# Expert weights in a fixed ring of eight buffers, context weights through GpSimd's queue, expert outputs combined by pairs

## The chip, the cores and the metric

The kernel runs on one core of a Trainium2 chip, in fp32. The metric is the device time of one execution in microseconds (us), as the median of several runs. TensorE (PE) has two clock levels, 1.2 and 2.4 GHz; the profile gives the granted clock of a stretch as a share of the upper one. PE's weight loads have an engine name of their own (PEld). DVE is VectorE, ACT is ScalarE, POOL is GpSimd, and SP is SyncE, which here only issues DMAs.

## What is computed

Two model blocks run one after the other on a latent sequence `x` and a context sequence `ctx_2` of 256 tokens each. The first block ends with a mixture of 32 experts, the second begins with a mixer that needs the projections of its own context. Cut to what matters here:

```python
def hier_moe(h, wg, bg, we, be, w_gate, w_up, w_down):     # 4 groups x 8 experts, top 2 of one group
    ...
    for gi in range(N_GROUPS):
        hid = (jax.nn.silu(jnp.einsum('td,edf->tef', t, w_gate[gi]))
               * jnp.einsum('td,edf->tef', t, w_up[gi])
               * combine[:, gi, :, None].astype(t.dtype))
        out = out + jnp.einsum('tef,efd->td', hid, w_down[gi])
    return out.reshape(B, L, D).astype(h.dtype)
...
# block 2, layer 0: the context's part does not depend on block 1
hc = modulate_2(rmsnorm(ctx, norm1_g[layer]), csh1, csc1)
cx = project_in(hc, w_in)
...
c_f, s_f = chunked_gated_linear_attention(cq, ck, cv, ca_f, zero, False)
```

The width is 1024, an expert's hidden width 512, and the 32 experts have 192 MB of fp32 weights, all of which are read.

## The kernel before

**The expert stage.** The function `moe` takes the 32 experts in 16 pairs `q`. The tokens of two pairs (a quad, `qd`) are gathered at once (`dispatch`). For a pair, `gate_up(q)` multiplies eight 1 MB chunks of gate and up weights, and `down(q - 1)` four chunks of the pair before; the two experts of a pair stand on the two halves of PE's columns, so their matmuls come in twos. Between its parts the code calls `step()`, which runs one piece of the list `todo` (gathering the next quad, adding up a finished one), and, for q > 0, `next(ctx, None)`.

**The context in between.** `ctx` is the generator `context()`: the context's part of block 2, layer 0. Each `yield` ends a piece, and one piece is run after each of the four sub-steps of a `gate_up`. It loads `ctx_2`, normalises and transposes it, and then multiplies it by nine blocks of `w_in_2` (1 MB where they have 256 columns, 512 KB where 128, 128 KB where 32). `weights_c` splits a block into a high and a low part, `whi` by a cast on ACT and `wlo` by a subtraction on DVE (`s.split`), and asks for the next one (`s.raw`). Then come four gated heads; each begins with a matmul `tr<-dTc,upst`, a chain of DVE and ACT operations that ends in `de`, one `yield`, and the transposes of `de`.

**Buffers and queues.** All 192 expert chunks are loaded by `chunk(i)` on SP's queue in a fixed order. A chunk goes to one of six buffers: three of the rotating pool buffers `raw`, another `raw` in `moe`'s own pool, and the two halves `rawh` of `h0`. The context's blocks are loaded by SP too, into the same three rotating `raw` buffers. SP works in order: a load whose buffer is not yet free holds up all that stand behind it.

**Adding up.** `down` leaves the outputs of two pairs in `yh` and `yl` (high and low part); `combine(qd)` multiplies them by the selection matrix in four parts of eight matmuls each and adds the result to `xT`, once for every two pairs. The parts stand at the end of `todo`.

Of the kernel before, what the change touches and what calls it, by code (L numbers as in the profile page):

```python
# [17 lines left out]
P = 128  # L18
D = 1024
# [999 lines left out]
def moe(s):  # L1019
    nc, tc, I = s.nc, s.tc, s.I  # L1020
    mt = nc.tensor.matmul
    CAP = s.cap
    with tc.tile_pool(name="pm", bufs=1) as pool_:
        pool = Pool(pool_, {"xg": 2, "raw": 1, "t1": 4, "kq": 4, "sel": 2, "selT": 3, "hT": 2, "ws": 4, "glo": 2, "sq": 2},
                    {"nt": "sq", "adarow2": "glo"})
# [109 lines left out]
        for _ in range(2):  # L1135
# [10 lines left out]
                 [(q - 1, u, j) for u in (4, 5) for j in range(2) if q > 0]]  # L1146
        first = [(s.wp, "raw")] * 3 + [(pool, "raw")] + [(s.wp, "whi"), (s.wp, "wlo")] * 2
        big = []

        def chunk(i):  # L1150

            if i >= 8:
                n = 4 + (i - 8) % 2 if i < 10 else (i - 10) % 6 if i < 184 else (i - 184) % 4
            if i < 8 or n < 4:
                p_, tag = first[i if i < 8 else n]
                t = p_.tile([P, 2048], F32, tag=tag, name="raw")
            else:

                if not big:
                    big.append(s.xp.tile([P, 2, 2048], F32, tag="h0", name="rawh"))  # L1160
                t = big[0][:, n - 4]
# [6 lines left out]
        pre = s.pre + [chunk(i) for i in range(3, 8)]  # L1168
        made = 8

# [49 lines left out]
        nc.vector.tensor_tensor(wsq[:, :, 1], s.fng, s.fng, op=OP.mult)  # L1220
        yh = pool.tile([P, 2, D], F32R, name="yh")
        yl = pool.tile([P, 2, D], F32R, tag="yl", name="yl")
        quads = {}
# [85 lines left out]
        def down(q, hT, then):  # L1309
            i = q % 2  # L1310
# [12 lines left out]
            for c in range(2):  # L1323
                sl = slice(512 * c, 512 * c + 512)
                nc.scalar.copy(yh[:, i, sl], pd[c])
                nc.vector.tensor_tensor(yl[:, i, sl], pd[c], yh[:, i, sl], op=OP.subtract)

        def combine(qd):
            _, selT, _ = quads.pop(qd)

            def part(c):
                po = s.at((P, 2, T))
                for j in range(2):
                    sl = slice((c + j) * P, (c + j + 1) * P)
                    for y in (yh, yl):
                        for i in range(2):
                            mt(po[:, j], y[:, i, sl], selT[:, i], start=y is yh and i == 0, stop=y is yl and i == 1)
                for j in range(2):
                    s.hold = nc.vector.scalar_tensor_tensor(s.xT[:, c + j], po[:, j], s.gt2[:, c + j:c + j + 1],
                                                            s.xT[:, c + j], op0=OP.mult, op1=OP.add).ins  # L1340
                if qd == 7:

# [15 lines left out]

            return [lambda c=c: (last if qd == 7 else part)(c) for c in range(0, 8, 2)]

# [5 lines left out]
        def load_context():  # L1366
            s.ctx2 = s.raw(I["ctx_2"][0].rearrange("(a p) d -> p a d", p=P))
# [4 lines left out]
        def context():  # L1372


            load_context()
            kb = pool.tile([P, 512], F32, name="kbc")
# [36 lines left out]
            cols += [(3072, 256), (3328, 256)]  # L1413
            raws = [s.raw(w2[:, :, c:c + n]) for c, n in cols[:1]]

            def weights_c():

                w = s.split(None, raws.pop(0))
                cols.pop(0)
                if cols:  # L1420
                    raws.append(s.raw(w2[:, :, cols[0][0]:cols[0][0] + cols[0][1]]))
                return w

# [24 lines left out]
            for hp in range(2):  # L1448
# [12 lines left out]
                for j in range(2):  # L1461
# [30 lines left out]
                    nc.vector.tensor_tensor(cu, cu, kst, op=OP.mult)  # L1492
                    yield
                    pt = s.tr((P, 4, P))
# [21 lines left out]
                    for i in range(4):  # L1516
                        for d in range(2):
# [41 lines left out]
        for q in range(17):  # L1559
# [11 lines left out]
            if q == 16:  # L1571
# [571 lines left out]
```

## Time and profile before

| | |
|---|---|
| median of 3 runs | 2094.33 us (2093.67 to 2095.58) |
| the profiled execution: own time | 2095.14 us |
| its span in the profile | 2093.4 us |
| granted clock over the span | 0.975 |
| PE busy | 1973.5 us (94%) |
| DVE, ACT busy | 1156.8 us (55%), 742.1 us (35%) |
| HBM read | 431.10 MB |

The expert stage lies between 428 and 1010 us from the span's start, the mixer of block 1 ahead of it and block 2 behind it. The profiled execution's own time is 1.74 us above its span.

### The profile page before, as it was taken

What the parts mean: (1) busy time and instruction counts of PE and PEld (TensorE: products, weight loads), DVE (VectorE), ACT (ScalarE), POOL (GpSimd) and SP (SyncE); (2) the same over time, 40 slices, a digit from 0 to 9 for tenths busy, and PEclk for the clock granted to TensorE, in tenths of its full rate; (3) what the DMA queues carried; (4) which work ended last, traced back from release to release, by engine and by line L of the source; (5) the groups of instructions that cost most, each with busy time, mean ns of one, the idle gap of its engine ahead of it and who ended that gap; (6) DMA issues with size and microseconds to landing.
All of it is one profiled execution on the core that took longest, in us unless ns stands there. A gap on an engine that the chain in (4) does not pass through costs nothing.

```text
span 2093.4 us, 28360 instructions
## 1 busy us (share of the span) xinstructions
PE 1973.5 (94%) x11684; PEld 1460.8 (70%) x11684; DVE 1156.8 (55%) x2161; ACT 742.1 (35%) x1117; POOL 9.9 (0%) x32
## 2 busy tenths in 40 slices
PE   6998989998989999998899999999999989998998
PEld 2766779744534444433678889787788977988998
DVE  5768785512132231111477997674734658787555
ACT  2564544422232231101353344222313444444444
POOL 0000000000000000000000000000000000000000
PEclk9999999999999999999889999999999999999999
DMA  8525556769788779999634352543433242466552
GB/s 283 173 98 186 166 176 239 250 255 374 272 330 330 308 296 370 377 423 409 210 115 149 123 181 68 175 161 116 148 100 99 66 141 84 159 222 201 182 182 101
DMA packets 228700, 434.02 MB, mean 207 GB/s; under 512 B 18347, under 2 KB 162824, under 8 KB 203736
## 3 DMA queue, kind: packets, MB, share of 16 engines
q1 hardware_dynamic: 218248, 427.22, 57.4%
q10 hardware_dynamic: 10192, 4.87, 0.9%
q8 instruction: 93, 1.52, 0.3%
q14 instruction: 39, 0.32, 0.0%
q0 software_dynamic: 128, 0.08, 0.0%
HBM read 431.10 MB, written 1.05 MB: 206 GB/s over the span
## 4 chain that ended last, share of the span: by engine, by line
PE 44%; DVE 4%; ACT 2%; issue 0%; DMA 0%; DVEq 0%; ACTq 0%
PE mm L226 13%; PE mm L227 13%; PE mm L228 13%; PE tr L296 1%; DVE wlo L216 1%; PE at L1893 1%; PE at L1887 0%; DVE nt L366 0%; DVE hc L371 0%; ACT whi L215 0%; DVE acc L289 0%; DVE sx L1805 0%; PE tr L1850 0%; PE at L1879 0%; PE at L1897 0%
## 5 line engine op out<-in xcount | busy, mean ns | idle before, releaser
L216 DVE TENSOR_TENSOR wlo<-raw,whi 128x2048 fp32r<-128x2048 f32 (+2 forms) x147 | 318.2, 2164 | 183.2 <-ACT whi L215 183.0
L226 PE MATMUL mm<-hh,whi 128*128 128x256 f32 (+2 forms) x1232 | 405.8, 330 | 6.3 <-DVE sq L2071 2.4
L228 PE MATMUL mm<-hh,wlo 128*128 128x256 f32 (+2 forms) x1232 | 400.7, 326 | 9.2 <-DVE wlo L216 9.2
L215 ACT CAST whi<-raw 128x2048 fp32r<-128x2048 f32 (+2 forms) x147 | 265.2, 1804 | 354.0 <-PE mm L227 293.5
L227 PE MATMUL mm<-hc,whi 128*128 128x256 f32 (+2 forms) x952 | 314.1, 330 | 0.2
L226 PEld LDWEIGHTS mm<-hh,whi 128*128 128x128 f32 (+1 forms) x1232 | 235.3, 191 | 31.8 <-issue 5.5
L228 PEld LDWEIGHTS mm<-hh,wlo 128*128 128x128 f32 (+1 forms) x1232 | 235.3, 191 | 31.0 <-DVE wlo L216 10.7
L289 DVE SCALAR_TENSOR_TENSOR acc<-raw,sc,acc 128x512 f32<-128x512 f32 x308 | 219.2, 745 | 14.2 <-DMA raw<-in_ada_w_dram 12.7
L227 PEld LDWEIGHTS mm<-hc,whi 128*128 128x128 f32 (+1 forms) x952 | 180.5, 190 | 18.3 <-issue 2.6
L226 PE MATMUL mm<-hidh,whi 128*128 128x256 f32 (+1 forms) x544 | 178.6, 331 | 0.0
L228 PE MATMUL mm<-hidh,wlo 128*128 128x256 f32 (+1 forms) x544 | 177.9, 330 | 0.1
L227 PE MATMUL mm<-hidl,whi 128*128 128x256 f32 (+1 forms) x544 | 177.2, 328 | 0.0
L1287 PE MATMUL mm<-raw,xg 128*64 128x512 f32 x544 | 144.7, 620 | 14.2 <-DMA raw<-in_moe_w_up_dram 11.9
L226 PE MATMUL mm<-whi,hh 128*128 128x256 f32 x448 | 134.2, 300 | 5.3 <-ACT vr L1704 2.7
L1287 PE MATMUL mm<-rawh,xg 128*64 128x512 f32 x480 | 131.0, 598 | 7.7 <-DMA rawh<-in_moe_w_up_dram 6.2
L227 PE MATMUL mm<-wlo,hh 128*128 128x256 f32 x448 | 132.5, 296 | 5.3 <-DVE wlo L216 5.3
L228 PE MATMUL mm<-whi,hc 128*128 128x256 f32 x448 | 133.7, 299 | 1.8 <-DVE hc L371 1.8
L227 PEld LDWEIGHTS mm<-hidl,whi 128*128 128x128 f32 x544 | 102.3, 188 | 11.2 <-DVE hidl L221 0.8
L228 PEld LDWEIGHTS mm<-hidh,wlo 128*128 128x128 f32 x544 | 101.8, 188 | 10.8 <-DVE wlo L216 0.7
L226 PEld LDWEIGHTS mm<-hidh,whi 128*128 128x128 f32 x544 | 101.7, 188 | 10.9 <-ACT hidh L220 0.9
L1287 PEld LDWEIGHTS mm<-raw,xg 128*64 128x64 f32 x544 | 42.1, 142 | 89.0 <-issue 66.5
L227 PE MATMUL mm<-hl,whi 128*128 128x256 f32 (+1 forms) x320 | 100.0, 313 | 0.0
(577 smaller groups left out, 2990.1 us busy)
## 6 DMA issues: line engine op xcount, KB each, us to landing
raw<-in_ada_w_dram SPq DMA_DIRECT2D x68, 1024.0 KB, 5.3
raw<-in_moe_w_down_dram SPq DMA_DIRECT2D x64, 1024.0 KB, 7.6
raw<-in_w_mlp_dram SPq DMA_DIRECT2D x64, 1024.0 KB, 5.3
raw<-in_w_in_dram SPq DMA_DIRECT2D x52, 1024.0 KB, 5.9
raw<-in_moe_w_gate_dram SPq DMA_DIRECT2D x34, 1024.0 KB, 7.4
raw<-in_moe_w_up_dram SPq DMA_DIRECT2D x34, 1024.0 KB, 7.0
rawh<-in_moe_w_gate_dram SPq DMA_DIRECT2D x30, 1024.0 KB, 9.5
rawh<-in_moe_w_up_dram SPq DMA_DIRECT2D x30, 1024.0 KB, 7.5
```

Of the source, the lines that this page charges most:

```text
L215: self.nc.scalar.copy(hv, v)
L216: self.nc.vector.tensor_tensor(lv, v, hv, op=OP.subtract)
L226: mt(out, ah, bh, start=first, stop=False)
L227: mt(out, ah, bl, start=False, stop=False)
L228: mt(out, al, bh, start=False, stop=last)
L289: nc.vector.scalar_tensor_tensor(acc[:, i], v[:, kk], s[:, k:k + 1], acc[:, i], op0=OP.mult, op1=OP.add)
L296: nc.tensor.matmul(pt[:n, :P], self.hot[:, 15 - r:15 - r + n], acc[:, r // 4, (r % 4) * P:(r % 4 + 1) * P], start=r == 0, stop=r == n - 1)
L1287: mt(pg[64 * j:64 * j + 64], xg[:, k, 2 * i + j], vs[j][:, kk], start=k == 0, stop=k == 7)
L1893: mt(po[:, 2 * g + t], sc[:, a, t * P:(t + 1) * P], vr[:, 2 * g + a, h * P:(h + 1) * P], start=a == 0, stop=g == 1 and a == 1)
```

## The change

The expert chunks get fixed buffers: the three that were loaded ahead, two (rather than one) in `moe`'s pool, one `wlo` buffer, and, from chunk 9 on, the two halves of `h0`: a ring of eight, taken in turn up to chunk 183, and then six. Three further buffers are used once at the start. One of these, `split_raw`, becomes the only buffer for `ctx_2` and the nine blocks of `w_in_2`; they are loaded by GpSimd's queue and split into one pair of buffers, `whc` and `wlc`. Outputs are added up after each pair: `combine(q)` has four parts of four matmuls, put at the front of `todo`. `yh` and `yl` hold one pair instead of two. Each head of the context has three more `yield`s.

```diff
-        first = [(s.wp, "raw")] * 3 + [(pool, "raw")] + [(s.wp, "whi"), (s.wp, "wlo")] * 2
-        big = []
+        new = lambda p_, tag: p_.tile([P, 2048], F32, tag=tag, name="raw")
+        ring = [v.rearrange("p k c -> p (k c)") for v in s.pre] + [new(pool, "raw") for _ in range(2)]
+        once = [new(s.wp, "whi"), new(s.wp, "wlo"), new(s.wp, "whi")]
+        split_raw = once[2]
+        ring.append(new(s.wp, "wlo"))
+        once = ring + once
         def chunk(i):
-            if i >= 8:
-                n = 4 + (i - 8) % 2 if i < 10 else (i - 10) % 6 if i < 184 else (i - 184) % 4
-            if i < 8 or n < 4:
-                p_, tag = first[i if i < 8 else n]
-                t = p_.tile([P, 2048], F32, tag=tag, name="raw")
...
+            if i == len(once):
+                big = s.xp.tile([P, 2, 2048], F32, tag="h0", name="rawh")
+                ring.extend(big[:, n] for n in range(2))
+                once.extend(ring[-2:])
+            t = once[i] if i < 11 else ring[(i - 11) % 8] if i < 184 else ring[(i - 184) % 6]
...
-        yh = pool.tile([P, 2, D], F32R, name="yh")
-        yl = pool.tile([P, 2, D], F32R, tag="yl", name="yl")
+        y2 = pool.tile([P, 2, D], F32R, tag="yl", name="y2")
+        yh, yl = y2[:, 0], y2[:, 1]
...
-        def combine(qd):
-            _, selT, _ = quads.pop(qd)
+        def combine(q):
+            selT = quads[q // 2][1][:, q % 2]
+            if q % 2:
+                quads.pop(q // 2)
             def part(c):
                 po = s.at((P, 2, T))
                 for j in range(2):
                     sl = slice((c + j) * P, (c + j + 1) * P)
-                    for y in (yh, yl):
-                        for i in range(2):
-                            mt(po[:, j], y[:, i, sl], selT[:, i], start=y is yh and i == 0, stop=y is yl and i == 1)
+                    mt(po[:, j], yh[:, sl], selT, start=True, stop=False)
+                    mt(po[:, j], yl[:, sl], selT, start=False, stop=True)
...
         def context():
-            load_context()
+            s.ctx2 = split_raw.rearrange("p (a d) -> p a d", a=2)
+            nc.gpsimd.dma_start(s.ctx2, I["ctx_2"][0].rearrange("(a p) d -> p a d", p=P))
...
-            raws = [s.raw(w2[:, :, c:c + n]) for c, n in cols[:1]]
+            split_h = s.wp.tile([P, 2048], F32R, tag="whi", name="whc")
+            split_l = s.wp.tile([P, 2048], F32R, tag="wlo", name="wlc")
+            def ask():
+                n = cols[0][1]
+                v = split_raw[:, :8 * n].rearrange("p (k c) -> p k c", c=n)
+                nc.gpsimd.dma_start(v, w2[:, :, cols[0][0]:cols[0][0] + n])
+                return v
+            asked = [ask()]
             def weights_c():
-                w = s.split(None, raws.pop(0))
+                v = asked.pop(0)
...
+                nc.scalar.copy(hv, v)
+                nc.vector.tensor_tensor(lv, v, hv, op=OP.subtract)
                 cols.pop(0)
                 if cols:
-                    raws.append(s.raw(w2[:, :, cols[0][0]:cols[0][0] + cols[0][1]]))
-                return w
+                    asked.append(ask())
+                return hv, lv
...
                     nc.vector.tensor_tensor(cu, cu, kst, op=OP.mult)
-                    yield
+                    for _ in range(3):
+                        yield
                     pt = s.tr((P, 4, P))
...
                                                            pk[a_ % 2][ps_, a_ // 2], op0=OP.mult, op1=OP.add)
+                    yield
                     yield
                     po = s.at((P, 4, P))
...
-            if q % 2 == 0:
-                todo += combine(q // 2 - 1)
+            todo[:0] = combine(q - 1)
+            if q == 16:
                 step()
```

**On SP's queue** (the DMAs in the order in which SP issues them, here at pair 4; L1164 is the load of an expert chunk, L175 that of a context block) there stands before:

```order
L1164 DMA rawh<-in_moe_w_up_dram 128x2048 x2
L175 DMA raw<-in_w_in_dram 128x8x256 x2
L1164 DMA raw<-in_moe_w_down_dram 128x2048 x4
L1164 DMA rawh<-in_moe_w_gate_dram 128x2048 x2
L1164 DMA raw<-in_moe_w_gate_dram 128x2048 x2
L175 DMA raw<-in_w_in_dram 128x8x32
L1164 DMA raw<-in_moe_w_up_dram 128x2048 x2
L1164 DMA rawh<-in_moe_w_up_dram 128x2048 x2
L175 DMA raw<-in_w_in_dram 128x8x128
```

Of the change, SP at about the same place, where L1165 is the load of an expert chunk:

```order
L1165 DMA raw<-in_moe_w_gate_dram 128x2048 x4
L1165 DMA raw<-in_moe_w_up_dram 128x2048
L1165 DMA rawh<-in_moe_w_up_dram 128x2048 x2
L1165 DMA raw<-in_moe_w_up_dram 128x2048
L1165 DMA raw<-in_moe_w_down_dram 128x2048 x4
```

And GpSimd's queue, which has none of these loads before:

```order
L1377 DMA raw<-in_ctx_dram 128x2x1024
L1422 DMA raw<-in_w_in_dram 128x8x256 x2
L1422 DMA raw<-in_w_in_dram 128x8x32
L1422 DMA raw<-in_w_in_dram 128x8x128 x4
L1530 MEMSET sxc 64x128
L1531 MEMSET sxc 64x128
```

SP is left with the expert chunks alone; the ten context loads moved to GpSimd, all into one buffer.

**On PE, at the first product of a context block** (L226 to L228 is such a product, of three matmuls for each eighth of the block; L1287 or L1288 is an expert's gate and up, L1319 its down), there stands before:

```order
L1319 MATMUL mm<-raw,hT 64x512 x2
L1319 MATMUL at<-raw,hT 64x512 x2
L1287 MATMUL mm<-rawh,xg 64x512 x7
L1287 MATMUL mm<-raw,xg 64x512 x16
L1287 MATMUL mm<-rawh,xg 64x512 x8
L1304 MATMUL tr<-kres,glo 128x128 x4
L226 MATMUL mm<-whi,hc 128x256
L227 MATMUL mm<-wlo,hc 128x256
```

Of the change, from the last transposes of `ctx_2` (L1400) on; L1337 and L1338 are the matmuls that add up outputs:

```order
L1400 MATMUL tr<-kres,raw 128x128 x4
L1288 MATMUL mm<-raw,xg 64x512
L1337 MATMUL at<-selT,y_3802 128x256
L1338 MATMUL at<-selT,y_3802 128x256
...
L1288 MATMUL mm<-rawh,xg 64x512
L1288 MATMUL mm<-raw,xg 64x512
L1288 MATMUL mm<-rawh,xg 64x512
L1288 MATMUL mm<-raw,xg 64x512
L1288 MATMUL mm<-rawh,xg 64x512
L1288 MATMUL mm<-raw,xg 64x512
L1288 MATMUL mm<-rawh,xg 64x512 x2
L226 MATMUL mm<-whc,hc 128x256
```

The rows left out are six more of L1337 and L1338. Between the transposes that read `split_raw` and the product that needs the first block from it stand nine expert matmuls and eight that add up; before, the block had a buffer of its own and was asked for earlier.

**On PE, at the chain of a head** (L1465 before, L1480 in the change, begins it; L1496 before, L1512 in the change, needs its end `de`), there stands before:

```order
L1465 MATMUL tr<-dTc,upst 128x256
L1319 MATMUL mm<-raw,hT 64x512
L1319 MATMUL at<-raw,hT 64x512
L1319 MATMUL mm<-raw,hT 64x512 x2
L1319 MATMUL at<-raw,hT 64x512 x2
L1319 MATMUL mm<-raw,hT 64x512
L1319 MATMUL at<-raw,hT 64x512
L1496 MATMUL tr<-kres,de 128x128 x2
```

Of the change, with L1480 some 90 rows ahead of these:

```order
L1258 MATMUL tr<-identr,sel 128x128 x2
L1263 MATMUL tr<-comb,sel 64x1 x4
L1337 MATMUL at<-selT,y_3802 128x256
L1338 MATMUL at<-selT,y_3802 128x256
L1288 MATMUL mm<-raw,xg 64x512
L1337 MATMUL at<-selT,y_3802 128x256
L1338 MATMUL at<-selT,y_3802 128x256
L1512 MATMUL tr<-kres,de 128x128 x2
L1520 MATMUL at<-ec,cu 128x128 x4
```

Eight expert matmuls stood between the two; now it is two whole sub-steps more.

## Rows read from the trace of the kernel before

**Rows 1.** Windows of the expert stage; columns: us, busy (count) by engine, PEclk, DMA, GB/s.
```profile
428.00:450.00 22.00, 22.00 (x131) 11.06 (x130) 3.90 (x17) 10.41 (x24) 0.00 (x0) 1.00 0.63 245
450.00:858.00 408.00, 378.45 (x1873) 182.63 (x1874) 104.50 (x244) 102.97 (x192) 1.20 (x6) 0.97 0.85 325
858.00:1010.00 152.00, 139.68 (x616) 54.77 (x612) 18.00 (x33) 18.78 (x33) 0.00 (x0) 1.00 0.99 405
```
**Rows 2.** Weight loads of PE, 428 to 1010 us: busy, mean ns, then idle time by releaser.
```profile
L1287 PEld LDWEIGHTS mm<-raw,xg 128*64 128x64 f32 x512 | 39.9, 143 | 85.6 <-issue 63.1 <-DMA raw<-in_moe_w_up_dram 16.1 <-DMA raw<-in_moe_w_gate_dram 3.0
L1287 PEld LDWEIGHTS mm<-rawh,xg 128*64 128x64 f32 x480 | 38.5, 137 | 69.7 <-issue 50.5 <-DMA rawh<-in_moe_w_up_dram 12.7 <-DMA rawh<-in_moe_w_gate_dram 2.2
L1319 PEld LDWEIGHTS mm<-raw,hT 128*64 128x64 f32 x256 | 21.6, 138 | 36.8 <-issue 22.8 <-DMA raw<-in_moe_w_down_dram 10.1 <-ACT yh L1325 0.7
L1337 PEld LDWEIGHTS at<-selT,yh 128*128 128x128 f32 x114 | 18.4, 189 | 15.5 <-issue 9.1 <-ACT yh L1325 5.7 <-DVE xT L1339 0.7
L1496 PEld LDWEIGHTS tr<-kres,de 128*128 128x128 f32 x8 | 0.9, 156 | 14.3 <-DVE de L1490 14.3
```
**Rows 3.** The same view, 858 to 1010 us.
```profile
L1287 PEld LDWEIGHTS mm<-rawh,xg 128*64 128x64 f32 x144 | 11.4, 136 | 26.4 <-issue 14.4 <-DMA rawh<-in_moe_w_up_dram 9.1 <-DMA rawh<-in_moe_w_gate_dram 2.2
L1287 PEld LDWEIGHTS mm<-raw,xg 128*64 128x64 f32 x138 | 10.8, 137 | 23.6 <-issue 16.9 <-DMA raw<-in_moe_w_up_dram 3.3 <-DMA raw<-in_moe_w_gate_dram 3.0
L1319 PEld LDWEIGHTS mm<-raw,hT 128*64 128x64 f32 x96 | 8.4, 135 | 16.7 <-DMA raw<-in_moe_w_down_dram 8.0 <-issue 6.7 <-ACT yh L1325 0.7
```
**Rows 4.** Waits of SP's queue, 450 to 858 us: total us, times, longest.
```profile
SPq L1164 <- PE mm L1287: 155.9, 46, 13.8
SPq L1164 <- DVE wlo L216: 41.2, 8, 14.7
```
**Rows 5.** Timeline of SP at 689 us: start, us.
```profile
689.29 15.37 SPq L1164 DMA_DIRECT2D raw<-in_moe_w_up_dram  x2
```
**Rows 6.** Timeline of PE, 560 to 612 us; a program matmul has two records.
```profile
587.39 3.69 PE L1287 MATMUL mm<-rawh,xg 128*64 128x512 f32 x16
...
602.03 0.44 PE L1496 MATMUL tr<-kres,de 128*128 128x128 f32 x2 [4.15 <-DVE de L1490]
602.40 1.95 PE L1319 MATMUL mm<-raw,hT 128*64 128x512 f32 x4
604.11 1.94 PE L1319 MATMUL at<-raw,hT 128*64 128x512 f32 x4
```
**Rows 7.** DMA issues, 428 to 1010 us: count, KB each, median us to landing.
```profile
raw<-in_w_in_dram SPq DMA_DIRECT2D x6, 1024.0 KB, 8.4
```
**Rows 8.** DMA queues, 116 to 120 us (packets, MB, share), and a load on GpSimd's queue.
```profile
q0 software_dynamic: 32, 0.05, 5.1%
...
prow<-in_ada_b_dram POOLq DMA_DIRECT2D x1, 48.0 KB, 2.1
```
**Rows 9.** DMA queues, 402.5 to 404 us: packets, MB, share of 16 engines.
```profile
q1 hardware_dynamic: 70, 0.55, 86.4%
q10 hardware_dynamic: 71, 0.07, 13.3%
```
**Rows 10.** Groups of DVE and ACT, 428 to 1010 us.
```profile
L215 ACT CAST whi<-raw 128x2048 fp32r<-128x2048 f32 x4 | 7.6, 1900 | 8.2 <-DMA raw<-in_w_in_dram 8.2
L216 DVE TENSOR_TENSOR wlo<-raw,whi 128x2048 fp32r<-128x2048 f32 x4 | 9.2, 2290 | 1.5 <-ACT whi L215 1.5
L1339 DVE SCALAR_TENSOR_TENSOR xT<-at,gt,xT 128x256 f32<-128x256 f32 x56 | 24.7, 479 | 34.0 <-PE at L1337 32.8
```
**Rows 11.** Timeline of PE at 570 us.
```profile
570.35 0.28 PE L227 MATMUL mm<-hc,whi 128*128 128x256 f32 x1
570.47 0.28 PE L228 MATMUL mm<-hc,wlo 128*128 128x256 f32 x1
...
570.68 1.07 PE L1287 MATMUL mm<-raw,xg 128*64 128x512 f32 x2
571.68 0.39 PE L226 MATMUL mm<-hc,whi 128*128 128x256 f32 x1
```

More of the change, by code (lines that the diff above doesn't have):

```diff
@@ L1023, in moe @@
     with tc.tile_pool(name="pm", bufs=1) as pool_:
-        pool = Pool(pool_, {"xg": 2, "raw": 1, "t1": 4, "kq": 4, "sel": 2, "selT": 3, "hT": 2, "ws": 4, "glo": 2, "sq": 2},
+        pool = Pool(pool_, {"xg": 2, "raw": 2, "t1": 4, "kq": 4, "sel": 2, "selT": 3, "hT": 2, "ws": 4, "glo": 2, "sq": 2},
                     {"nt": "sq", "adarow2": "glo"})
@@ L1146, in moe @@
                  [(q - 1, u, j) for u in (4, 5) for j in range(2) if q > 0]]
-        first = [(s.wp, "raw")] * 3 + [(pool, "raw")] + [(s.wp, "whi"), (s.wp, "wlo")] * 2
-        big = []
-        def chunk(i):
-            if i >= 8:
-                n = 4 + (i - 8) % 2 if i < 10 else (i - 10) % 6 if i < 184 else (i - 184) % 4
-            if i < 8 or n < 4:
-                p_, tag = first[i if i < 8 else n]
-                t = p_.tile([P, 2048], F32, tag=tag, name="raw")
[L1157 to L1161, printed above, removed]
+        new = lambda p_, tag: p_.tile([P, 2048], F32, tag=tag, name="raw")
[4 more added lines that the diff above has]
+        once = ring + once
+        def chunk(i):
+            if i == len(once):
[3 more added lines that the diff above has]
+            t = once[i] if i < 11 else ring[(i - 11) % 8] if i < 184 else ring[(i - 184) % 6]
             src = s.expert_w(*order[i])
@@ L1165, in chunk @@
             return v
-        pre = s.pre + [chunk(i) for i in range(3, 8)]
-        made = 8
+        pre = s.pre + [chunk(i) for i in range(3, 9)]
+        made = 9
         def weights():
@@ L1309, in down @@
         def down(q, hT, then):
-            i = q % 2
             pd = [s.mm(), s.at()]
@@ L1324, in down @@
                 sl = slice(512 * c, 512 * c + 512)
-                nc.scalar.copy(yh[:, i, sl], pd[c])
-                nc.vector.tensor_tensor(yl[:, i, sl], pd[c], yh[:, i, sl], op=OP.subtract)
-        def combine(qd):
-            _, selT, _ = quads.pop(qd)
+                nc.scalar.copy(yh[:, sl], pd[c])
+                nc.vector.tensor_tensor(yl[:, sl], pd[c], yh[:, sl], op=OP.subtract)
+        def combine(q):
+            selT = quads[q // 2][1][:, q % 2]
+            if q % 2:
+                quads.pop(q // 2)
             def part(c):
@@ L1340, in part @@
                                                             s.xT[:, c + j], op0=OP.mult, op1=OP.add).ins
-                if qd == 7:
+                if q == 15:
                     if c == 0:
@@ L1357, in last @@
                         s.vg2.append(s.split(w2[:, :, 2560 + 256 * len(s.vg2):2816 + 256 * len(s.vg2)]))
-            return [lambda c=c: (last if qd == 7 else part)(c) for c in range(0, 8, 2)]
+            return [lambda c=c: (last if q == 15 else part)(c) for c in range(0, 8, 2)]
         w2 = I["w_in_2"][0].rearrange("(k p) c -> p k c", p=P)
@@ L1413, in context @@
             cols += [(3072, 256), (3328, 256)]
-            raws = [s.raw(w2[:, :, c:c + n]) for c, n in cols[:1]]
-            def weights_c():
-                w = s.split(None, raws.pop(0))
+            split_h = s.wp.tile([P, 2048], F32R, tag="whi", name="whc")
[6 more added lines that the diff above has]
+            asked = [ask()]
+            def weights_c():
+                v = asked.pop(0)
+                hv, lv = [t[:, :v.shape[1] * v.shape[2]].rearrange("p (k c) -> p k c", k=8)
+                          for t in (split_h, split_l)]
+                nc.scalar.copy(hv, v)
+                nc.vector.tensor_tensor(lv, v, hv, op=OP.subtract)
                 cols.pop(0)
                 if cols:
-                    raws.append(s.raw(w2[:, :, cols[0][0]:cols[0][0] + cols[0][1]]))
-                return w
+                    asked.append(ask())
+                return hv, lv
             def product(w, m):
```

## The prediction

> **What bounds the kernel now.** The change acts in the expert stage, so I first cut the span there and read windows [rows 1]. From 428 to 1010 us (582 us) the kernel moves 245 x 22 + 325 x 408 + 405 x 152, about 199.6 MB. At the rate of the last stretch (405 GB/s at a DMA share of 0.99, so 409) that would take 488 us. The stage thus lies 94 us above its DMA floor. The reader is to see that the limit changes inside it: from 450 to 858 PE is busy for 378 of 408 us and DMA has a share of 0.85; from 858 on DMA is full and PE waits.
>
> What a change can take away here is PE's own waits, read from the groups of its weight loads, where a late operand shows [rows 2]. Expert chunks that came late cost 16.1 + 3.0 + 12.7 + 2.2 + 10.1 = 44.1 us. The same view from 858 on holds 9.1 + 2.2 + 3.3 + 3.0 + 8.0 = 25.6 of it [rows 3], so 18.5 lie before. The transposes of `de` wait 14.3 us [rows 2], in three of the four heads.
>
> Why are chunks late before 858 with DMA idle 15% of the time? SP's waits answer [rows 4]. Waits on PE (155.9 us in 46) are a full ring and harmless. But eight waits on `wlo` take 41.2 us: a chunk stands in line for a rotating buffer that a context block must leave by being split. One of them held SP for 15.4 us [rows 5].
>
> A stall of PE costs a second time. After the 4.15 us wait for `de`, two rows of four records start 1.71 us apart; sixteen records at full pace take 3.69, 0.92 for four [rows 6]. PE ran on its lower clock level there. The granted clock of 0.97 over 408 us [rows 1] bounds this at 0.03 x 408, 12 us.
>
> **What goes.** (a) SP no longer waits for a split: it issues only expert chunks, into eight buffers. The 18.5 us before 858 go. (b) The 25.6 us after it go if DMA is less behind by then. The context's pieces end in pair 13 rather than 10 (49 pieces instead of 37, counted in PE's order, four to a pair), so PE work moves from the early, PE-bound pairs to the late, DMA-bound ones while the ring stays full. I count both, 44.1, and charge below what may be left. (c) Two sub-steps more stand between the start of a head's chain and its transposes; one holds at least eight matmuls, 8 x 0.46 (3.69 / 8 [rows 6]) = 3.7 us, and the largest wait shown is 4.15. The 14.3 us go. (d) Half-clock time after these stalls: between 0 and 12, I take 5. Together **63.4 us**.
>
> **What comes.** No context load by GpSimd's queue stands in this trace, so its time has bounds from rows. A 1 MB block alone: 2.56 us at 409 GB/s and the 2.1 us that a small load took on that queue [rows 8], 4.7. Beside a busy SP queue packets go one for one: at 403 us 70 packets of SP's queue and 71 of another left in the same 1.5 us [rows 9], that is 1.5 x 16 / 70 = 0.34 us on an engine for a pair. A block of 256 columns is 1024 rows of 1 KB. The small load's 48 KB (96 rows of 512 B) went in at most 32 packets [rows 8], three rows or more to one; so 341 packets, 21 to an engine, 21 x 0.34 + 2.1 = 9.4 us. With one row to a packet it is 64 x 0.34 + 2.1 = 24 us. SP's own took 8.4 [rows 7]. I take 8 for 1 MB and 6 for 512 KB: nearest to the middle bound, as the queue's own row has several rows to a packet, and SP's queue is not always busy.
>
> The Trainium skill ("DMA: Bandwidth & Descriptors", Queues, rings and completion order) says that each DMA engine goes round the queue rows packet by packet. The 70 to 71 above agrees. What it makes of the time depends on the packet's size alone; its outcome is the slower rival below.
>
> - *`ctx_2`*: asked for when chunk 8 has been used, with little expert work before the squares and the row sums that PE transposes for. 0 to 12; 4.
> - *First block*: one buffer, so it is asked for only after the last transposes of `ctx_2`. PE then has nine expert matmuls at 0.46 and eight of the adding-up at 0.12 (the pace of such matmuls, 570.35 to 570.47 [rows 11]), 5.1 us. 8 + 1.9 for the cast [rows 10] - 5.1, about 5.
> - *Later blocks*: each is asked for after the split of the one before. PE work in between, from its order: 26 us (second), 13 (third), 11 (fourth), 3.7 (fifth), 100 (sixth), 7.7 (seventh). Only the fifth is uncovered: 6 + 1.0 - 3.7, about 3. A split also waits for the product before it (one pair of buffers), 0 to 2 us each; that is in the range.
> - *Half clock after these stalls*: 0 to 12 as above; 5.
> - *Adding up each pair*: the wait on `yh` was 5.7 us for eight rounds [rows 2], now sixteen with at least eight matmuls between; 0 to 11.4, I take 5. The 256 matmuls stay. 64 more additions of 0.479 us [rows 10] are 31 us of DVE, hidden: DVE is busy 104.5 of 408 us [rows 1]. Without that cover all 31 would count.
> - *Cut pairs of expert matmuls*: by PE's order 52 odd cuts instead of 44. A lone matmul holds PE 1.00 us (570.68 to 571.68) [rows 11], against 0.46 in a pair; 8 x 0.54, about 4.
> - *Chunk waits left*: pairs 14 to 16 have no context work; there 12 chunks of 2.56 us each pass 31 us a pair, against about 26 of PE, and eight buffers hold 20 us of lead. 0 to 18.5; 8.
> - *Tail*: `load_context` at the end waits for chunk 190 instead of 188, and its transposes stand inside the last adding-up; that itself has half the matmuls. 0 to 3 either way; 0.
>
> Sum 4 + 5 + 3 + 5 + 5 + 4 + 8 = 34. Net 63.4 - 34 = 29.4, so 2095.14 - 29.4 = 2065.7 for the profiled execution. The median lies 0.8 below that one: **2065**.
>
> One rule of the skill speaks against the change: "SBUF — State Buffer" (SBUF: two separate sides) warns that DMAs issued from GpSimd's queue starve while DVE runs an operation that takes the port pair which both share. No run here shows it. DVE's longest in the stage is 2.29 us [rows 10]; once on each of the three exposed loads that is 7 us, 2072, inside the forecast's range.
>
> **Rivals.** *Slower: the loads by GpSimd starve* (one row to a packet, 24 us each beside a busy SP). For it: the one-for-one row [rows 9], and that SP now always has chunks to send. Against it: the small load's 32 packets [rows 8], and that SP's queue pauses when its ring is full, 155.9 us of waits [rows 4]. Price, from the PE work listed above and a cast of 1 to 1.9 us: first 20.8, fifth 21.3, seventh 17.3, fourth 14.0, third 11.4, together 85 instead of 8, so 77 more. SP runs out of free buffers while PE waits and leaves the queue to the load, so I take two thirds: 51, about 2116. The sign turns where the sum reaches 8 + 29.4, at a load of 15 us (11.8 + 12.3 + 8.3 + 5.0 + 2.4 = 39.8).
>
> *No change, about 2094*: the new waits come out at twice what I took (68 against 63), or the 25.6 us after 858 stay because the stage stays DMA-bound there. For it: DMA at 0.99 [rows 1]. Against it: the 15% idle DMA before 858, which a ring of eight can use.
>
> *More, about 2040*: no new wait shows. `ctx_2`, the first and fifth block, the half clock and `yh` cost nothing (4 + 5 + 3 + 5 + 5 = 22), and 2 to 3 of the other terms go. For it: SP's waits for a full ring [rows 4], which leave the DMA engines to GpSimd's load; 4.7 us alone is within the 5.1 us of cover.
>
> **How the numbers follow.** Forecast 0.55, its own range 2046 to 2082 (the half-clock, `ctx_2` and `yh` terms to their ends). More gain 0.18, no change 0.09, slower by starving loads 0.18. 2030 to 2104 leaves out most of the last and the edge of the second, 2 in 10. About 0.2% (4 us) is what a measurement of this kernel can tell from no change. The forecast and the larger gain are faster, as is a small part of the third: 0.75. Same 0.08. Slower 0.17.
>
> **What would show it.** SP's waits on `wlo` gone (a); PE's waits on expert chunks down from 44 us to under 15, also late in the stage (b); no wait at L1512 on `de` (c); granted clock at 0.97 or above between 450 and 858 (d). GpSimd's loads landing in 6 to 9 us, and waits of L226 on `whc` under 10 us in all; 15 us or more there and the slower rival is right. I am wrong as well if the stage is no shorter than 582 us with chunk waits gone: then PE's work itself grew.

## The result, and the profile after

The changed kernel takes 2061.56 us (median of four runs, 2060.20 to 2066.89), the kernel before 2094.95 on the same chip. The ratio is 0.9843, with a 95% interval of 0.9822 to 0.9864. The profiled execution is the slowest of the four (2066.89 us, span 2065.1); the same program profiled once more, below, has 2058.61.

All of it is in the expert stage. From pair 0's activation to the last expert matmul it took 581.5 us before (428.1 to 1009.6) and 552.0 after (430.1 to 982.1). Ahead of it 2 us were lost, behind it nothing changed (1083.7 against 1082.8 us).

The windows of the changed kernel, with the columns of [rows 1]:

```profile
450.00:858.00 408.00, 388.47 (x1928) 181.90 (x1924) 121.37 (x290) 107.91 (x202) 9.18 (x15) 0.98 0.91 358
858.00:982.00 124.00, 121.28 (x586) 53.50 (x586) 27.44 (x56) 19.06 (x32) 0.00 (x0) 1.00 0.93 365
```

PE is busy for 388 us where it was for 378, DMA's share rose from 0.85 to 0.91, and the stretch in which DMA was full and PE waited is gone: PE is busy for 121 of the last 124 us.

The waits of PE's weight loads, same stretch of work as [rows 2], now by the view of waits (engine, line, releaser: us in total, times, longest):

```profile
PEld mm L226 <- ACT whc L1432: 13.2, 2, 11.0
PEld at L1337 <- ACT y L1325: 10.5, 9, 2.1
PEld at L1337 <- DVE xT L1340: 4.6, 7, 0.8
PEld at L351 <- DVE cd L348: 3.3, 1, 3.3
PEld at L1338 <- DVE y L1326: 1.8, 5, 0.4
PEld mm L1319 <- DMA raw<-in_moe_w_down_dram: 1.5, 1, 1.5
PEld mm L1288 <- DMA raw<-in_moe_w_up_dram: 1.4, 1, 1.4
```

The waits on expert chunks fell from 44.1 to 2.9 us. The wait on `de` (L1496 in [rows 2], 14.3) is gone; the row of its transposes now has no idle time:

```profile
L1512 PEld LDWEIGHTS tr<-kres,de 128*128 128x128 f32 x8 | 1.0, 138 | 0.0
```

These are waits of weight loads, and they are not yet time that PE lost: a load can wait while PE still works on matmuls that were loaded before it. The same view for PE's matmuls gives the idle time of PE itself, first before, then in the changed kernel:

```profile
PE mm L1287 <- DMA raw<-in_moe_w_up_dram: 11.9, 6, 3.7
PE tr L1496 <- DVE de L1490: 11.5, 4, 4.6
PE mm L1287 <- DMA rawh<-in_moe_w_up_dram: 6.2, 6, 1.3
PE mm L1319 <- DMA raw<-in_moe_w_down_dram: 3.0, 6, 0.6
...
PE mm L226 <- ACT whc L1432: 11.4, 2, 10.1
PE at L1337 <- ACT y L1325: 3.0, 3, 1.2
PE mm L1319 <- DMA raw<-in_moe_w_down_dram: 0.6, 1, 0.6
PE mm L1288 <- DMA raw<-in_moe_w_up_dram: 0.5, 1, 0.5
```

With 3.4 us more on gate chunks, PE stood idle for chunks for 24.5 us before and 1.1 after, and for `de` for 11.5 and 0.

In their place stand one wait of 11.0 us for the first context block (L226; 10.1 on PE) and waits for `y`, the outputs of one pair. SP now waits for a full ring and little else; `wlo` and `wlc` do not occur among the waits of its expert loads ([rows 4] has the shorter stretch from 450 to 858 us; here it is 450 to 982):

```profile
SPq L1165 <- PE mm L1288: 294.3, 102, 15.7
SPq L1165 <- PE at L1319: 99.0, 34, 8.0
```

The context's loads on GpSimd's queue (count, KB each, median us to landing), which [rows 7 and 8] could only bound:

```profile
raw<-in_w_in_dram POOLq DMA_DIRECT2D x4, 1024.0 KB, 11.1
raw<-in_w_in_dram POOLq DMA_DIRECT2D x4, 512.0 KB, 5.6
raw<-in_ctx_dram POOLq DMA_DIRECT2D x1, 1024.0 KB, 7.6
```

The first block's load was issued at 480.91 us; this is when ACT could split it and PE could go on (start, us, idle before):

```profile
493.93 1.90 ACT L1432 CAST whc<-raw 128x2048 fp32r<-128x2048 f32 x1 [12.12 <-DMA raw<-in_w_in_dram]
...
495.88 0.58 PE L226 MATMUL mm<-whc,hc 128*128 128x256 f32 x1 [10.15 <-ACT whc L1432]
```

13.0 us passed from issue to split. The window around it, in the columns of [rows 1], is the one place of the stage with a clearly lower clock:

```profile
480.00:500.00 20.00, 9.85 (x37) 3.62 (x39) 6.00 (x11) 3.69 (x5) 1.81 (x2) 0.70 0.87 351
```

### The profile page after: what moved, and what is told of

It reads as the page before. It is cut to its first block, busy times and chain, and to the rows that moved or that the text cites. A ratio compares the mean times of both kernels' runs of the same rounds, so it can differ in the third digit from the quotient of the medians.

```text
span 2065.1 us, 28445 instructions
## 1 busy us (share of the span) xinstructions
PE 1961.6 (95%) x11684; PEld 1456.8 (71%) x11684; DVE 1181.7 (57%) x2225; ACT 742.1 (36%) x1117; POOL 18.7 (1%) x42
## 4 chain that ended last, share of the span: by engine, by line
PE 67%; DVE 6%; ACT 3%; DMA 2%; issue 1%; DVEq 0%; ACTq 0%
PE mm L226 14%; PE mm L227 14%; PE mm L228 13%; PE mm L1288 11%; PE mm L1319 2%; PE at L1319 2%; PE at L1251 2%; PE tr L296 1%; DVE wlo L216 1%; PE at L1337 1%; PE at L1338 1%; DMA raw<-in_moe_w_up_dram 1%; DMA raw<-in_w_in_dram 1%; PE at L1910 1%; ACT whi L215 1%
## 5 line engine op out<-in xcount | busy, mean ns | idle before, releaser
L226 PE MATMUL mm<-hh,whi 128*128 128x256 f32 (+2 forms) x1232 | 407.2, 331 | 7.0 <-DVE sq L2088 2.4
L228 PE MATMUL mm<-hh,wlo 128*128 128x256 f32 (+2 forms) x1232 | 402.1, 327 | 8.9 <-DVE wlo L216 8.9
L216 DVE TENSOR_TENSOR wlo<-raw,whi 128x2048 fp32r<-128x2048 f32 (+2 forms) x138 | 303.7, 2200 | 161.3 <-ACT whi L215 161.0
L215 ACT CAST whi<-raw 128x2048 fp32r<-128x2048 f32 (+2 forms) x138 | 253.1, 1834 | 347.0 <-PE mm L227 298.0
L227 PE MATMUL mm<-hc,whi 128*128 128x256 f32 (+3 forms) x912 | 303.5, 333 | 0.1
L226 PEld LDWEIGHTS mm<-hh,whi 128*128 128x128 f32 (+1 forms) x1232 | 236.5, 192 | 32.5 <-issue 5.5
L228 PEld LDWEIGHTS mm<-hh,wlo 128*128 128x128 f32 (+1 forms) x1232 | 236.5, 192 | 30.7 <-DVE wlo L216 10.2
L1288 PE MATMUL mm<-raw,xg 128*64 128x512 f32 x784 | 243.0, 601 | 0.5 <-DMA raw<-in_moe_w_up_dram 0.5
L289 DVE SCALAR_TENSOR_TENSOR acc<-raw,sc,acc 128x512 f32<-128x512 f32 x308 | 219.3, 746 | 14.1 <-DMA raw<-in_ada_w_dram 12.6
L227 PEld LDWEIGHTS mm<-hc,whi 128*128 128x128 f32 (+1 forms) x912 | 174.5, 191 | 17.4 <-issue 1.8
L226 PE MATMUL mm<-hidh,whi 128*128 128x256 f32 (+1 forms) x544 | 178.8, 331 | 0.0
L228 PE MATMUL mm<-hidh,wlo 128*128 128x256 f32 (+1 forms) x544 | 177.3, 329 | 0.1
L1288 PEld LDWEIGHTS mm<-raw,xg 128*64 128x64 f32 x784 | 70.1, 137 | 96.7 <-issue 90.4
L226 PE MATMUL mm<-whi,hh 128*128 128x256 f32 x448 | 132.7, 297 | 5.1 <-ACT vr L1721 2.5
L228 PE MATMUL mm<-whi,hc 128*128 128x256 f32 x384 | 113.6, 296 | 1.8 <-DVE hc L371 1.8
L228 PEld LDWEIGHTS mm<-hidh,wlo 128*128 128x128 f32 x544 | 102.1, 189 | 11.0 <-DVE wlo L216 0.7
L227 PEld LDWEIGHTS mm<-hidl,whi 128*128 128x128 f32 x544 | 102.0, 188 | 11.1 <-DVE hidl L221 0.8
L226 PEld LDWEIGHTS mm<-hidh,whi 128*128 128x128 f32 x544 | 101.6, 188 | 10.8 <-ACT hidh L220 0.9
L1288 PE MATMUL mm<-rawh,xg 128*64 128x512 f32 x240 | 106.7, 609 | 0.0
```

Of the source, the lines that this page charges most:

```text
L215: self.nc.scalar.copy(hv, v)
L216: self.nc.vector.tensor_tensor(lv, v, hv, op=OP.subtract)
L226: mt(out, ah, bh, start=first, stop=False)
L227: mt(out, ah, bl, start=False, stop=False)
L228: mt(out, al, bh, start=False, stop=last)
L289: nc.vector.scalar_tensor_tensor(acc[:, i], v[:, kk], s[:, k:k + 1], acc[:, i], op0=OP.mult, op1=OP.add)
```

## The experiments

The twelve runs below have four to six executions each, beside the kernel before on the same chip (medians 2095 to 2098); the first two rows are the kernels compared above. "Chunk waits" are those of weight loads. The last four columns take the stage apart on PE, by the starts of its records: the time in which PE stood idle, the part of it that ended with a chunk, the time on expert matmuls, and what the lower clock added (half of PE's working time at that level; the other columns hold the rest of it). What is not listed, mostly the adding up and the context's matmuls, is 142 to 150 us in every run.

Where every expert matmul runs together with its partner on the other half of PE's columns, expert matmuls take 336 us (the last three rows). A matmul that runs alone adds 0.43 us, so the kernel before has some 110 of 768 alone and the changed one some 100.

| run | median us | ratio, 95% interval | stage us | chunk waits us | PE idle | of it chunks | expert matmuls | lower clock |
|---|---|---|---|---|---|---|---|---|
| before | 2094.33 | | 581.5 | 44.1 | 41.9 | 24.5 | 384.6 | 11.3 |
| changed | 2061.56 | 0.9843 (0.9822 to 0.9864) | 552.0 | 2.9 | 22.2 | 1.1 | 378.6 | 3.0 |
| changed, once more | 2060.65 | 0.9820 (0.9803 to 0.9836) | 547.5 | 3.1 | 18.9 | 1.0 | 378.9 | 1.6 |
| context on SP | 2063.38 | 0.9841 (0.9820 to 0.9862) | 549.9 | 10.1 | 12.4 | 4.8 | 386.3 | 1.7 |
| old yields | 2072.16 | 0.9878 (0.9856 to 0.9901) | 559.0 | 7.8 | 22.6 | 3.5 | 382.8 | 5.0 |
| ring of six | 2072.69 | 0.9885 (0.9865 to 0.9906) | 561.0 | 15.5 | 21.3 | 5.6 | 388.6 | 2.3 |
| ring of six, context on SP | 2071.74 | 0.9863 (0.9846 to 0.9879) | 561.1 | 24.8 | 18.2 | 10.9 | 389.9 | 3.4 |
| the same, old yields | 2091.57 | 0.9970 (0.9957 to 0.9984) | 578.5 | 26.7 | 28.7 | 12.4 | 393.1 | 6.8 |
| before, new yields | 2082.23 | 0.9916 (0.9900 to 0.9933) | 569.4 | 33.9 | 29.7 | 25.9 | 386.3 | 11.7 |
| before, adding up by pairs | 2104.74 | 1.0042 (1.0026 to 1.0059) | 592.4 | 35.2 | 39.2 | 23.7 | 389.1 | 15.8 |
| early block | 2060.26 | 0.9824 (0.9802 to 0.9845) | 547.5 | 2.8 | 10.5 | 1.1 | 384.7 | 3.2 |
| whole pairs | 2051.60 | 0.9783 (0.9761 to 0.9804) | 540.4 | 3.7 | 46.5 | 5.8 | 336.2 | 11.2 |
| early block, whole pairs | 2042.45 | 0.9743 (0.9722 to 0.9764) | 528.3 | 2.7 | 37.3 | 5.8 | 335.8 | 7.2 |
| the same, two waits mended | 2026.46 | 0.9669 (0.9650 to 0.9687) | 514.2 | 2.8 | 25.4 | 8.0 | 335.4 | 8.2 |

The scheduler orders PE's work anew for every edit, and the expert matmuls' time moves with that order by up to 14 us between runs that leave the pairs free. A run's time is therefore not the price of its edit alone.

### Which queue: the context's loads on SP

```diff
-            nc.gpsimd.dma_start(s.ctx2, I["ctx_2"][0].rearrange("(a p) d -> p a d", p=P))
+            nc.sync.dma_start(s.ctx2, I["ctx_2"][0].rearrange("(a p) d -> p a d", p=P))
...
-                nc.gpsimd.dma_start(v, w2[:, :, cols[0][0]:cols[0][0] + n])
+                nc.sync.dma_start(v, w2[:, :, cols[0][0]:cols[0][0] + n])
```

> The changed kernel with its ten context loads issued by SP instead of GpSimd, into the same fixed buffer. My theory (SP held up by a split makes expert chunks late): SP shows waits on wlc or on the transposes again, 20 to 60 us in all; PE's waits on expert chunks rise from 2.9 us to 8 to 20 us; the first block comes sooner (8 us instead of 13), which gives 3 to 5 us back; time 2062 to 2076. Rival (GpSimd's slow loads cost more than SP's order; the ring of eight alone removed the chunk waits): chunk waits stay under 5 us, time 2050 to 2058.

SP waited 59.5 us for splits, more than the 41.2 us of [rows 4]:

```profile
SPq L1422 <- DVE wlc L1433: 59.5, 5, 22.5
```

Yet the time is 2063.4, 2 to 3 us above the changed kernel, with intervals that overlap. PE's chunk waits rose from 2.9 to 10.1 us, as my theory had it, and the wait on the first block (13.2 us on `whc`) fell to 0.6: SP's loads of 1 MB took 5.2 us in the median. On PE these two do not balance: its idle time is 6.5 us less than in the changed kernel once more, though 3.8 us more of it ends with a chunk. The expert matmuls, in another order of PE, took the gain back with 7.4 us more. So the choice of the queue made no difference to the time; what it is worth with PE's order held was not run.

### How deep: a ring of six

```diff
-            t = once[i] if i < 11 else ring[(i - 11) % 8] if i < 184 else ring[(i - 184) % 6]
+            t = once[i] if i < 11 else ring[(i - 11) % 6] if i < 184 else ring[(i - 184) % 6]
```

> The changed kernel with the expert chunks in turn over six of the eight buffers (the two halves of h0 are used once). If depth is what absorbs the uneven pairs: PE's waits on chunks rise from 2.9 us to 10 to 25 us, time 2070 to 2085. If it was only SP's wait for the split that made chunks late: chunk waits under 6 us, time 2061 to 2066.

Time (2072.7 us) and chunk waits (15.5) are as expected of depth, with SP's queue as free of context loads as in the changed kernel:

```profile
PEld mm L1288 <- DMA raw<-in_moe_w_up_dram: 9.8, 8, 2.2
PEld mm L1319 <- DMA raw<-in_moe_w_down_dram: 5.7, 8, 1.4
```

But the waits do not make up the time. Against the changed kernel once more PE idles 4.6 us longer for chunks, 2.4 longer in all; of the 13.5 us by which the stage is longer 9.7 are expert matmuls, more of which ran alone. That depth keeps chunk waits off PE is shown; how much of the 11 us is depth and how much PE's order is not.

Both edits together (ring of six and the loads on SP):

> The changed kernel with both the ring of six and the context loads on SP. My theory (a queue held up by splits matters when the ring is shallow, and the ring of eight covered it in the run with SP): more than the sum of the two single runs (2072.7 and 2063.4 against 2061.6), PE's chunk waits 25 to 40 us, time 2080 to 2092. Rival (the two do not interact): chunk waits 16 to 24 us, 2072 to 2077.

The time, 2071.7, says the rival: no worse than the ring of six alone. Chunk waits did grow (24.8 us, just above the rival's range; on PE from 5.6 to 10.9), but the first block's wait is gone here too. With six buffers as with eight the queue changes the kind of wait and not the time.

### When: the heads' yields

The changed kernel with the old number of yields, and the kernel before with the new one; the edit of the second is this, the first is its reverse:

```diff
                     nc.vector.tensor_tensor(cu, cu, kst, op=OP.mult)
-                    yield
+                    for _ in range(3):
+                        yield
...
                                                            pk[a_ % 2][ps_, a_ // 2], op0=OP.mult, op1=OP.add)
+                    yield
                     yield
```

> The changed kernel without the three added yields of each head. My theory (the yields take away the wait on de, and spread the context's work over the pairs that DMA bounds): waits on de of 10 to 16 us are back at the heads' transposes, and chunk waits late in the stage of 5 to 20 us, as context work ends in pair 10; time 2075 to 2095. Rival (the ring alone did it, the yields moved nothing): 2060 to 2066.

2072.2 us, a little below the expected range: waits on `de` of 7.0 us in two heads (5.3 on PE), where 10 to 16 were expected. Against the changed kernel once more PE idles 2.5 us longer for chunks, expert matmuls take 3.9 us more, and the lower clock costs 3.4 more.

> The kernel before with only the three added yields of each head. My theory: the 14.3 us of waits on de go, and later context work takes part of the 25.6 us of late chunk waits away; rotating buffers and SP's waits on wlo stay: time 2075 to 2085, chunk waits 30 to 42 us. Rival (without deeper buffers the yields only move the stall to late chunks): 2088 to 2096, chunk waits 50 us or more.

2082.2 us, in the range of my theory, but only its first half holds. No wait on `de` is left, and that is 11.5 of the 12.2 us by which PE's idle time fell. The chunk waits of weight loads went from 44.1 to 33.9, but PE itself idled no less for chunks: 25.9 us against 24.5, from 858 on 10.7 against 11.7. SP's waits on `wlo`, which I expected to stay, fell from 41.2 to 18.8 us between 450 and 858. The ring is still the old one. The yields by themselves are worth 12 to 18 us (2094.3 and 2098.1 for the kernel before, and the ratio).

With the ring of six, the loads on SP and the old yields, only the fixed buffers and the adding up by pairs are left of the change:

> The changed kernel with the ring of six, the context loads on SP and the heads' old yields: what is left of the change is fixed buffers and adding up by pairs. If the three parts carry the gain: 2088 to 2098, with waits on de of 7 to 15 us and chunk waits of 30 us or more. Rival (fixed buffers and the separate context buffer carry much of it): 2075 to 2085.

2091.6 us, ratio 0.9970: on the way from here to the changed kernel, the ring's depth and the yields carry the gain. The yields are worth 20 us in this setting (2091.6 against 2071.7), 11 us with eight buffers. Of the 17.4 us by which the stage is shorter, 10.4 are PE's idle time for `de` and 1.5 for chunks; expert matmuls and the lower clock make some 3 each. That the yields gain by spreading the context's work, the other half of my theory, these numbers hardly show.

### The price: adding up by pairs

The kernel before with `y2`, `combine(q)` and `todo[:0] = combine(q - 1)` of the change, and nothing else:

> The kernel before with only the adding up after each pair (half-sized yh and yl, parts at the front of the list). My theory: it costs by itself, since yh is waited for twice as often: waits on yh and yl of 12 to 22 us instead of 8, time 2095 to 2105; its worth is the buffer that it frees. Rival (shorter rounds even out the pairs): 2085 to 2092.

It costs 8 to 9 us (2104.7, ratio 1.0042), in the expected range, but not by the expected mechanism. The weight loads' waits on the outputs are 11.9 us, about the lower end:

```profile
PEld at L1337 <- ACT y L1325: 10.1, 8, 4.3
PEld at L1338 <- DVE y L1326: 1.8, 6, 0.3
```

PE itself idled for less time than before (39.2 us against 41.9). What grew is its working time: the matmuls that add up outputs took 37.5 us instead of 32.9, the expert matmuls 4.5 us more, and the lower clock cost 4.5 more. In the change this part leaves free 8 KB per partition, the size of one ring buffer, as `yh` and `yl` are half-sized; whether that buffer is worth the price was not run.

Between this run and the last one of the section before lie the fixed buffers, with a buffer of its own for the context: from a ratio of 1.0042 to 0.9970, 15 us. PE's idle time for chunks fell there from 23.7 to 12.4 us, more than in any other step. That run shows little gain over the kernel before because the adding up costs more than half of what the fixed buffers bring.

### The first block earlier

```diff
-        split_raw = once[2]
+        ctx_raw, split_raw = once[0], once[2]
...
-            s.ctx2 = split_raw.rearrange("p (a d) -> p a d", a=2)
+            s.ctx2 = ctx_raw.rearrange("p (a d) -> p a d", a=2)
             nc.gpsimd.dma_start(s.ctx2, I["ctx_2"][0].rearrange("(a p) d -> p a d", p=P))
...
+            asked = [ask()]
```

> The changed kernel with ctx_2 loaded into another buffer (the first whi buffer, later whc), so that the first block of w_in_2 can be asked for at once behind it instead of after the last transposes of ctx_2. My theory: the 11.0 us wait of the first product and the stretch at the lower clock behind it go, time 2046 to 2053. Rival (GpSimd's loads and expert chunks only change places: the earlier load makes chunks late or the wait moves to the second block): 2057 to 2062.

> The changed kernel once more, beside the three others. Its profiled execution was 5 us above its median, the early block gave only 1.3 us by the medians. If the first block's load takes varying time: the wait of the first product is clearly under 11 us here (4 to 8) and the profiled execution lies within 2 us of the median. If the wait is fixed: 10 to 12 us again, and the early block's gain went elsewhere. Time 2060 to 2064.

A puzzle. The wait on the first block is gone (2.1 us on `whc` are left), and the time is the same, 2060.3 against 2060.7. Nor was the wait a chance of one execution: the changed kernel once more has 10.5 us there. DMA did not take it back, chunk waits are 2.8 us. What differs is the order of PE. A `down` of the early block near 495 us:

```profile
494.95 1.07 PE L1319 MATMUL mm<-raw,hT 128*64 128x512 f32 x2
495.86 1.02 PE L1319 MATMUL at<-raw,hT 128*64 128x512 f32 x2
```

and one of the changed kernel once more, near 500 us:

```profile
499.45 1.08 PE L1319 MATMUL mm<-raw,hT 128*64 128x512 f32 x4
500.36 1.03 PE L1319 MATMUL at<-raw,hT 128*64 128x512 f32 x4
```

Two records are one matmul, and one matmul alone holds PE as long (0.9 us) as two on the two halves of its columns. The early block's expert matmuls take 384.7 us, the changed kernel's 378.9: 6 us for 14 more that run alone. Another 1.6 us went at the lower clock, granted behind a 3.6 us wait on `cd` at 450 us, and 1.3 in the context's matmuls. That is the 8.4 us by which PE idles less. PE shows no gap for a matmul that runs alone; busy time only grows.

### Whole pairs

To test that, the two matmuls of a pair are kept next to each other: the second gets a higher priority and an order edge to the first, and the first also waits for the second one's chunk.

```diff
+        def pair(w, out, lhs, rhs, start, stop):
+            (v0, _), (v1, d) = w
+            a = mt(out[:64], lhs(0), rhs(v0), start=start, stop=stop).ins
+            if d is not None:
+                tc.add_manual_dep(a, d.name, mybir.DependencyInfo(mybir.DependencyClass.Sync,
+                                  mybir.DependencyReason.DATA), reason="pair")
+            with tc.high_priority(), tc.issue_after(a):
+                mt(out[64:], lhs(1), rhs(v1), start=start, stop=stop)
```

> The changed kernel with the two matmuls of an expert pair always next to each other in PE's order (the first one also waits for the second one's chunk). My theory: the run with the early block lost its 10 us again because PE's order there had more expert matmuls alone instead of in twos; some 170 records run 0.43 us apart instead of 0.21 in the changed kernel, so up to 37 us are to be had, of which late chunks take some back: time 2028 to 2045. Rival (the stage is held by DMA by now, and PE's gain turns into waits on chunks): chunk waits of 25 us or more, 2052 to 2062.

2051.6 us, 9 less, and less than I expected. All 384 pairs are whole, and expert matmuls take 42.7 us less. Of this 27.6 us came back as idle time of PE and 9.6 at the lower clock (the granted clock from 450 to 858 is 0.96, against 0.99 in the changed kernel once more). Chunk waits of loads stay at 3.7 us, and PE's idle time for chunks grew by 4.8, so DMA took little of it. PE stopped elsewhere: waits on `glo` went from 9.8 to 28.6 us (18.9 on PE), the first block's wait is 12.0.

> The early block together with whole pairs. If the order of PE is what ate the early block's 10 us: 7 to 12 us below the run with whole pairs alone, 2018 to 2036. If something else ate them: within 4 us of it.

2042.5 us, 9 below whole pairs alone. Expert matmuls take the same time in both (336.2 and 335.8 us), idle time is 9.2 us less and the lower clock costs 4.0 less: with the pairs held together, the early block is worth what it removes. The cause of the puzzle is shown.

What is left there is the wait on `glo`; the longest of its waits:

```profile
705.70 1.90 ACT L1439 CAST whc<-raw 128x2048 fp32r<-128x2048 f32 x1 [12.50 <-DMA raw<-in_w_in_dram]
...
710.98 1.13 PE L1313 MATMUL tr<-kres,glo 128*128 128x128 f32 x4 [9.29 <-DVE glo L1306]
```

The eighth context block, not needed before the last head is done, was asked for at 693.07 us and landed 12.6 us later. ACT's cast and DVE's subtraction for it stood ahead of `glo` in their engines' order, and PE waited for `glo`. A slow load thus stalls PE through two engines whose instructions stand in a fixed order. The last run puts that split behind the last head (`read` is the head's last copy) and the transposes of `glo` behind the first half of `down`:

```diff
-                        then()
+                        with tc.issue_after(one):
+                            then()
...
-                nc.scalar.copy(hv, v)
+                with tc.issue_after(read) if len(cols) == 2 else ExitStack():
+                    nc.scalar.copy(hv, v)
```

> Early block and whole pairs, with the two places mended at which the run with both showed PE waiting for glo (28.6 us): the transposes of glo stand behind the first half of down instead of ahead of it, and the eighth context block is split only after the last head. If those waits were on the path: 2018 to 2032, waits on glo under 8 us. Rival (DMA bounds the stage by now, at a share of 0.95): waits on chunks of 10 us or more take their place, 2036 to 2044.

2026.5 us, ratio 0.9669: both kernels are beaten, the changed one by 35 us. The windows:

```profile
450.00:858.00 408.00, 392.70 (x2152) 194.44 (x2153) 129.27 (x307) 113.30 (x211) 8.26 (x14) 0.98 0.97 384
858.00:942.00 84.00, 75.15 (x356) 29.27 (x354) 18.51 (x39) 10.10 (x14) 0.00 (x0) 1.00 0.95 388
```

The stage has 514 us, with 488 as its DMA floor by the prediction's sum. Waits of loads on `y` (25 us on ACT's half) are the largest left; on PE they are 11.3 us, and chunks 8.0.

## Why the prediction was right

The time (2061.6 against 2065) and the stage (29.5 us shorter in the profiled execution against 29.4) came out nearly as forecast, and what was forecast to go went: late chunks and the wait on `de`. That the sums agree so closely is luck. Single terms were off by 5 to 13 us in both directions, and one cause was given too large a part.

- **The size of what goes: the largest error.** The prediction reads 44.1 and 14.3 us from the groups of weight loads and calls them PE's own waits. PE itself idled for the same operands for 24.5 and 11.5 us. With 1.1 left, the chunks gave 23.4 us, where the sum has 44.1 less 8.
- **(a) SP's wait for splits: the step that did not hold as put.** The waits on `wlo` did go, and chunk waits with them. But with the loads back on SP and SP waiting 59.5 us for splits, PE idled only 3.8 us longer for chunks and the time was the same within its interval. The new yields in the kernel before halved SP's waits on `wlo`, and PE idled no less for chunks. The largest step came with the fixed buffers, which chunks do not share with the context (23.7 to 12.4 us on PE); depth and the queue took 4 to 6 us each, the yields at most 2.5. I read a wait of a queue as the cause of a late operand; it was a small part of it.
- **(b) Late chunks after 858: right that they go.** I charged 8 us as left; 2.9 were. The reason that I gave, context work moved to the late pairs, is not borne out: by itself it left PE 10.7 of 11.7 us idle there.
- **(c) The wait on `de`: right,** 14.3 to 0, on PE 11.5 to 0. (The view of waits has four of them, the longest 5.5 us, not three with 4.15 as I had it.)
- **(d) Half-clock time.** I had set 5 us won against 5 lost. The lower clock was granted for 27.3 us of the stage before and for 13.7 after. PE stood idle in much of the latter, so its cost fell from 11.3 to 3.0 us: 8 won on balance. The loss left lies in one place, around the first block's wait.
- **`ctx_2`:** 4 us taken; its one wait is 3.3, on PE 2.4.
- **First block: mis-sized,** 5 taken, 11.0 measured, on PE 10.1. Packets did go one for one beside SP's. From 486 to 488 us of the changed kernel (packets, MB, share; q1 is SP's queue, q0 GpSimd's):

```profile
q1 hardware_dynamic: 70, 0.51, 67.2%
q0 software_dynamic: 67, 0.27, 34.2%
```

  A packet of GpSimd's queue held 0.27 MB / 67, 4 KB: four rows, where my middle bound had three. That makes 256 packets for 1 MB, 16 to an engine, and by the prediction's formula 16 x 0.34 + 2.1 = 7.5 us. Two sizes were off: a pair of packets took 2 x 16 / 70 = 0.46 us, where the second packet of [rows 9] had 1 KB and not 4, and no packet of this load moved in the first 4 us after its issue. The Trainium skill ("DMA: Bandwidth & Descriptors", Queues, rings and completion order) has an engine go round its queue rows packet by packet, and in its section SWDGE vs HWDGE vs iDMA a packet of preferably no more than 4096 B; the 70 to 67 and the 4 KB agree with both.
- **Later blocks:** 3 taken, 2.2 on `whc` and 0.8 on `wlc` measured; 5.6 us for 512 KB against my 6.
- **Adding up: mis-sized,** 5 taken. Waits of loads on `y` are some 14 us in all against 8 before, and 7 against 1 fall on `xT`, DVE's addition; but PE idles for `y` for only some 4 us. What the sum put at nothing is PE's own time: the 256 matmuls stay, as it says, but took 38.4 us instead of 32.9. The 31 us of DVE's additions stayed hidden, as assumed.
- **Matmuls alone: the wrong sign.** 4 taken for cuts, but expert matmuls took 6 us less than before (378.6 against 384.6). My count of odd cuts in PE's order misled: it took two neighbouring matmuls for a pair whichever halves they use.

Against the sum, the chunks brought 13 us less and `de` 3 less, while the first block and the adding up cost about 5 more each. The other way went the cuts (10), the clock (8) and several small terms. They cancel.

The slower rival was wrong by its size: a load takes 5.6 (512 KB) and 11.1 us (1 MB) in the median, 13.5 at most, and not 24, though its mechanism, one packet for one, is seen. By the signs that the prediction set for itself the 1 MB loads landed late (it had 6 to 9 us) and L226 waited too long for `whc` (13.2 us; under 10 was the sign of being right, 15 or more that of the rival). The warning of the Trainium skill's page "SBUF — State Buffer" (SBUF: two separate sides) on GpSimd's DMAs behind DVE is not seen as a rule: of the changed kernel's ten loads one had its first packet 1.6 us after its issue with DVE busy for 0.8 us of them, another after 3.6 us with DVE idle throughout. The first block's load itself, with 4.1 us of which DVE was busy for 2.8, does not decide it.

## What to carry to other kernels

A queue that waits, or a weight load that waits, is not yet a loss: read the idle time of the engine itself (24.5 us of PE against 44.1 of its loads here), and test buffers, depth and queue apart. Where a chain of operations stands between two matmuls, put enough other work there: three yields in each head took away the wait on `de`, 10.4 and 11.5 us of PE in two of the settings and 5.3 in the third. After every edit under a scheduler, count the matmuls that run together: a gain that disappears without any new wait may have gone into busy time.

## What the runs showed of the hardware

- Two fp32 matmuls on the two column halves of PE run together only when one follows the other directly in PE's order; alone, one takes the 0.9 us of two. In the changed kernel some 100 of 768 run alone (379 us for the expert matmuls, 336 with the pairs held together), and holding the order took 9 us off, 18 together with the early block.
- Waits of PE's weight loads overstate what PE loses: for the expert chunks of the kernel before they add up to 44.1 us, with PE itself idle for 24.5.
- A load on GpSimd's queue moved its first packet 1.6 to 4.3 us after its issue; from the first to the last packet 1 MB then took from 3.4 us (45 packets of SP's queue went beside it) to 10.2 us (349). SP's loads of 1 MB blocks of `w_in_2` landed in 5.2 us in the median.
